# The sum S1 of two weight quadrants in a seven-product projection kernel: made on VectorE, or by an accumulating load

## The chip, the cores and the metric

The kernel runs on one core of a Trainium2 chip. The metric is device microseconds of one execution, the median of three runs.

## The reference, cut to what matters

One decoder layer: RMSNorm of `x`, one wide projection of it, four kinds of attention on parts of the projection, gates, four branch projections that are summed, an output projection and the residual. What matters for the change are the two large matrix products, with `w_in` (2048 x 20992) and with `w_out` (2048 x 2048):

```python
h = rms_norm(x, norm_g[l])
proj = jnp.einsum('bsd,de->bse', h, w_in[l])
(aq, ak, av, bq, bk, bv, cq, ck, cv, mq, za, zb, zc, zm, gates) = jnp.split(proj, split_at, axis=-1)
...
x = x + jnp.einsum('bsd,de->bse', merged, w_out[l])
```

## The kernel before

**Units.** Both products are done in units of 256 output columns, 82 for `w_in` and 8 for `w_out`; one call of `products` is one unit. A unit uses a scheme that needs seven block products instead of eight. Its weight is read as four quadrants of 128 x 1024 float32 (512 KB each): `a11`, `a21`, `a22`, `a12`. From these `wforms` makes the seven left operands: slot 1 is `a11`, slot 4 is S1 = `a21 + a22`, slot 5 is S1 minus `a11`, slot 6 is `a12` minus that, slot 0 is `a21 - a11`, slot 2 is `a12`, slot 3 is `a22`. S1 and its two successors are made in place in one buffer, so the operand for slot 4 has to be taken out before the one for slot 5 overwrites it, and so on.

**Split.** Each operand is split by `wsplit` into a rounded high part (ScalarE, line 135) and a low rest (VectorE, line 136). TensorE then does eight matmuls of the high part with 512 columns (line 612) and eight of the low part with 256 columns (line 615) for each slot. A slot of a unit is so 16 matmuls, a unit 112.

**Buffers.** The quadrants and S1 come from one pool of six buffers (`wraw`, `NW = 6`), five to a unit, handed out in turn. Each unit's S1 buffer is thus the one in which the unit before kept its `a12`, and it comes free when slot 2 of the unit before has been split. The split parts come from six buffers (`whl`, `NHL = 6`), so three splits may be ahead of TensorE.

**Queues.** The quadrants are loaded from SyncE's queue (line 579). GpSimd's queue carries the stores of results (`proj<-c` line 709, `gt<-c` and `sz<-c` line 720, `yz<-y` line 310, `out_dram<-c` line 801), some small loads, and short arithmetic of the attentions (`norms`, lines 247 to 251, and `rstd`, lines 148 and 149). VectorE also evacuates products (line 632), adds the parts of a result (line 651), scales gate columns (line 711) and adds the residual (line 800).

**Order.** The Tile framework's scheduler lays the instructions out engine by engine at build time, by priorities (`high_priority`) and its own timing model. At run time each engine goes through its list in order. Attention instructions stand among those of the units, so that TensorE has both.

Of the kernel before, what the change touches and what calls it, by code (L numbers as in the profile page):

```python
# [13 lines left out]
ALU = mybir.AluOpType  # L14
# [39 lines left out]
def trunk_kernel(ctx: ExitStack, tc: tile.TileContext, xT, xn, memT, memn, gains, wp, wmem,  # L54
                 wbA, wbB, wbC, wbM, wo, small_in, rows_in, tab, out):
    nc = tc.nc
    act, dve, pool, pe = nc.scalar, nc.vector, nc.gpsimd, nc.tensor
# [76 lines left out]
    def split(src, hi, lo):  # L134
        act.activation(hi, src, AF.Copy)  # L135
        dve.tensor_tensor(lo, src, hi.bitcast(F32), ALU.subtract)  # L136

    def wraw():
        return wst.tile([P, 1024], F32, name="wraw", bufs=NW)

    def wsplit(src):
        hi, lo = (wst.tile([P, 1024], F32R, name="whl", bufs=NHL) for _ in range(2))
        split(src, hi, lo)
        return hi, lo
# [429 lines left out]
    def wforms(src, early=False):  # L574

        with tc.high_priority(offset=AHEAD):
            a11, a21, a22, a12 = (wraw() for _ in range(4))
            for i, w in enumerate((a11, a21, a22, a12)):
                nc.sync.dma_start(w, src[:, i * 1024:(i + 1) * 1024])
            s1 = wraw()  # L580
            yield 1, wsplit(a11)
        with tc.high_priority(offset=AHEAD):
            dve.tensor_tensor(s1, a21, a22, ALU.add)  # L583
            dve.tensor_tensor(a21, a21, a11, ALU.subtract)  # L584
            yield 4, wsplit(s1)
        if early:
            with tc.high_priority(offset=AHEAD):
                yield 2, wsplit(a12)
        with tc.high_priority(offset=AHEAD):
            dve.tensor_tensor(s1, s1, a11, ALU.subtract)  # L590
            yield 5, wsplit(s1)
        with tc.high_priority(offset=AHEAD):
            dve.tensor_tensor(s1, a12, s1, ALU.subtract)  # L593
            yield 6, wsplit(s1)
        for slot_, w in ((0, a21), (2, a12), (3, a22)):
            if early and slot_ == 2:
                continue
            with tc.high_priority(offset=AHEAD):
                yield slot_, wsplit(w)

    def products(src, f, hq, last=None, phases=False, early=False):
# [7 lines left out]
        def mms(s, w, js, end):  # L609
# [4 lines left out]
            for j in js:  # L614
                pe.matmul(ps[:, 0:H], wl[:, j * P:(j + 1) * P], f[:, j, s, 0], start=False, stop=end and j == js[-1],  # L615
                          skip_group_check=s in (5, 6, 0, 3))

        ws = [v for v in wforms(src, early)]
        steps = [(v, range(8)) for v in ws]
        if early:  # L620
# [273 lines left out]
```

## Time and profile before

| what | value |
|---|---|
| median of 3 runs | 2290.77 us (2289.78 to 2290.8) |
| the profiled execution | 2289.92 us, its span 2288.1 us |
| granted TensorE clock, mean | 0.998 |
| TensorE busy | 2261.0 us, 99% |
| VectorE busy | 1870.5 us, 82% |
| ScalarE busy | 1273.8 us, 56% |
| GpSimd busy | 286.9 us, 13% |

The span is cut as follows: memory keys and the preparation of `x` up to about 61 us, the 82 units of `w_in` with the attentions among them up to about 1850 us, the branch projections, and the 8 units of `w_out` up to the end. In the profile an instruction is named by its line, engine, operation, the tile that it writes and those that it reads. "Idle before" is the time in which the engine had nothing to do just before the instruction, with what ended it.

### The profile page before, as it was taken

To read this page: it belongs to the slowest core of one execution; us is meant where nothing else is said; L and a number is where in the kernel's file an instruction comes from. 1 tells how busy PE (TensorE), PEld (TensorE's weight loads), DVE (VectorE), ACT (ScalarE), POOL (GpSimd) and SP (SyncE) were. 2 spreads that over 40 slices of the span, in tenths; PEclk is the share of its full clock that TensorE was granted. 3 is DMA by queue.
4 is the path that set the end of the run, shared out by engine and by line. 5 is a ranking of instruction groups with operands and counts; after the bars stand their busy time and mean duration, and the time that the engine had idled before them with its cause. 6 is when DMAs were issued, how large, how long until landed. Compare 5 with 4: busy or idle time off the path is not lost. (4 is left out here: it accounts for less than half of the span.)

```text
span 2288.1 us, 33763 instructions
## 1 busy us (share of the span) xinstructions
PE 2261.0 (99%) x12672; PEld 1951.3 (85%) x12672; DVE 1870.5 (82%) x2541; ACT 1273.8 (56%) x2253; POOL 286.9 (13%) x419
## 2 busy tenths in 40 slices
PE   9899999999999999999999999999999999999999
PEld 4788888888888888888888888888888888888888
DVE  5688899978887878888888888889888875578888
ACT  6646566675455456656666665656657542224444
POOL 2501011110011002111111201111021000010000
PEclk9999999999999999999999999999999999999999
DMA  8744444344443444444454434435344466485443
GB/s 302 231 139 139 138 151 158 125 143 133 139 129 118 131 165 135 157 130 152 141 158 135 153 125 157 137 128 159 111 157 137 144 214 215 157 278 176 138 164 113
DMA packets 114340, 355.43 MB, mean 155 GB/s; under 512 B 13744, under 2 KB 14256, under 8 KB 114176
## 3 DMA queue, kind: packets, MB, share of 16 engines
q1 hardware_dynamic: 95056, 287.89, 39.8%
q0 software_dynamic: 19120, 65.38, 7.7%
q8 instruction: 99, 1.62, 0.3%
q14 instruction: 65, 0.53, 0.1%
HBM read 294.47 MB, written 58.75 MB: 154 GB/s over the span
## 5 line engine op out<-in xcount | busy, mean ns | idle before, releaser
L612 PE MATMUL gbank<-f,whl 128*128 128x512 f32 x5040 | 1273.0, 396 | 15.5 <-ACT whl L135 10.6
L612 PEld LDWEIGHTS gbank<-f,whl 128*128 128x128 f32 x5040 | 913.7, 189 | 189.4 <-ACT whl L135 13.7
L135 ACT ACTIVATE whl<-wraw 128x1024 fp32r<-128x1024 f32 x678 | 706.2, 1057 | 497.0 <-PE gbank L612 159.6
L136 DVE TENSOR_TENSOR whl<-wraw,whl 128x1024 fp32r<-128x1024 f32 x678 | 821.2, 1220 | 167.0 <-ACT whl L135 161.4
L615 PEld LDWEIGHTS gbank<-f,whl 128*128 128x128 f32 x5040 | 677.3, 190 | 42.6 <-issue 1.0
L615 PE MATMUL gbank<-f,whl 128*128 128x256 f32 x5040 | 705.5, 284 | 0.0
L629 ACT ACTIVATE o<-gbank 128x512 f32<-128x512 f32 x270 | 159.8, 593 | 123.6 <-PE gbank L615 122.7
L632 DVE TENSOR_TENSOR o<-gbank,o 128x512 f32<-128x512 f32 x270 | 183.9, 686 | 27.0 <-PE gbank L615 19.9
L651 DVE TENSOR_TENSOR c<-o 128x512 f32<-128x512 f32 x179 | 132.5, 740 | 23.7 <-ACT o L634 23.4
L130 PE MATMUL gbank<-yz,whl 128*128 128x512 f32 x384 | 149.4, 389 | 0.0
L131 PE MATMUL gbank<-yz,whl 128*128 128x512 f32 x384 | 149.4, 389 | 0.0
L634 ACT ACTIVATE o<-gbank 128x512 f32<-128x512 f32 x89 | 52.8, 593 | 169.6 <-PE gbank L615 169.5
L132 PE MATMUL gbank<-yz,whl 128*128 128x512 f32 x384 | 147.0, 389 | 0.0
L583 DVE TENSOR_TENSOR wraw<-wraw 128x1024 f32<-128x1024 f32 x90 | 109.9, 1222 | 37.7 <-DMA wraw<-in_wp_dram 32.9
L593 DVE TENSOR_TENSOR wraw<-wraw 128x1024 f32<-128x1024 f32 x90 | 110.0, 1223 | 1.5
L590 DVE TENSOR_TENSOR wraw<-wraw 128x1024 f32<-128x1024 f32 x90 | 110.0, 1222 | 0.9
L584 DVE TENSOR_TENSOR wraw<-wraw 128x1024 f32<-128x1024 f32 x90 | 109.7, 1219 | 0.1
L131 PEld LDWEIGHTS gbank<-yz,whl 128*128 128x128 f32 x384 | 72.1, 188 | 15.1
L130 PEld LDWEIGHTS gbank<-yz,whl 128*128 128x128 f32 x384 | 72.1, 188 | 14.9
L132 PEld LDWEIGHTS gbank<-yz,whl 128*128 128x128 f32 x384 | 72.1, 188 | 14.8
L709 POOL DMA_DIRECT2D proj<-c x38 | 28.3, 746 | 442.8 <-DVE c L651 425.4
L720 POOL DMA_DIRECT2D gt<-c x32 | 24.5, 766 | 333.3 <-ACT c L718 282.9
(228 smaller groups left out, 1611.5 us busy)
## 6 DMA issues: line engine op xcount, KB each, us to landing
wraw<-in_wp_dram SPq DMA_DIRECT2D x328, 512.0 KB, 3.9
proj<-c POOLq DMA_DIRECT2D x38, 512.0 KB, 3.5
ld<-proj SPq DMA_DIRECT2D x76, 256.0 KB, 3.3
gt<-c POOLq DMA_DIRECT2D x32, 512.0 KB, 3.8
wraw<-in_wo_dram SPq DMA_DIRECT2D x32, 512.0 KB, 4.4
g<-gt SPq DMA_DIRECT2D x48, 256.0 KB, 4.0
wraw<-in_wmem_dram SPq DMA_DIRECT2D x16, 512.0 KB, 5.5
wraw<-in_wbB_dram SPq DMA_DIRECT2D x16, 512.0 KB, 4.2
```

The source lines that it names most:

```text
L130: pe.matmul(ps, ah, bh, start=first, stop=False)
L131: pe.matmul(ps, ah, bl, start=False, stop=False)
L132: pe.matmul(ps, al, bh, start=False, stop=last)
L135: act.activation(hi, src, AF.Copy)
L136: dve.tensor_tensor(lo, src, hi.bitcast(F32), ALU.subtract)
L590: dve.tensor_tensor(s1, s1, a11, ALU.subtract)
L593: dve.tensor_tensor(s1, a12, s1, ALU.subtract)
L612: pe.matmul(ps, wh[:, j * P:(j + 1) * P], f[:, j, s].rearrange("p a b -> p (a b)"), start=j == 0 and s in (1, 4, 2), stop=False, skip_grou ...
L615: pe.matmul(ps[:, 0:H], wl[:, j * P:(j + 1) * P], f[:, j, s, 0], start=False, stop=end and j == js[-1], skip_group_check=s in (5, 6, 0, 3))
L629: act.activation(q[{1: 0, 4: 3, 5: 1}[s]], ps, AF.Copy)
L632: dve.tensor_tensor(q[i], ps, q[i], ALU.add)
L651: dve.tensor_tensor(c, i0, i1, ALU.add)
```

## The change

S1 is no longer added up by VectorE from the two loaded quadrants. GpSimd loads `a21`'s columns a second time straight into the S1 buffer (the new line 581) and then `a22`'s columns a second time, with an accumulating load that adds them to what lies there (line 582). SyncE's four loads stay, since slots 0 and 3 need `a21` and `a22` by themselves. Later lines have numbers that are higher by one.

```diff
@@ -578,9 +578,10 @@
             for i, w in enumerate((a11, a21, a22, a12)):
                 nc.sync.dma_start(w, src[:, i * 1024:(i + 1) * 1024])
             s1 = wraw()
+            pool.dma_start(s1, src[:, 1024:2048])
+            pool.dma_start(s1, src[:, 2048:3072], accum_op=ALU.add)
             yield 1, wsplit(a11)
         with tc.high_priority(offset=AHEAD):
-            dve.tensor_tensor(s1, a21, a22, ALU.add)
             dve.tensor_tensor(a21, a21, a11, ALU.subtract)
             yield 4, wsplit(s1)
```

GpSimd's list before, in the columns of the A attention (`proj<-c` stores the result of a unit, the rows on `ssA` are the attention's arithmetic):

```order
L310 DMA yz<-y 128x512
L709 DMA proj<-c 128x2x512 x5
L247 TENSOR_TENSOR ssA<-ssA,r_101 128x8
L248 TENSOR_SCALAR ssA<-ssA 128x8
L250 TENSOR_TENSOR ssA<-ssA,hneg 128x8
L709 DMA proj<-c 128x2x512
L251 TENSOR_TENSOR ssA<-ssA,rA 128x8
```

The same engine and place in the changed kernel:

```order
L710 DMA proj<-c 128x2x512
L581 DMA wraw<-in_wp_dram 128x1024
L582 DMA wraw<-in_wp_dram 128x1024
L710 DMA proj<-c 128x2x512
L581 DMA wraw<-in_wp_dram 128x1024
L247 TENSOR_TENSOR ssA<-ssA,r_101 128x8
L248 TENSOR_SCALAR ssA<-ssA 128x8
L582 DMA wraw<-in_wp_dram 128x1024
L250 TENSOR_TENSOR ssA<-ssA,hneg 128x8
L251 TENSOR_TENSOR ssA<-ssA,rA 128x8
L710 DMA proj<-c 128x2x512
```

Between two stores there now stand the two loads of S1. Line 581 of a unit waits for VectorE's split of slot 2 of the unit before, line 582 for line 581's data. The store ahead of them is that of two units earlier, and in some units the attention's arithmetic stands between the two loads or behind them.

VectorE's list before, in the same columns, from line 590 of one unit to line 590 of the next:

```order
L590 TENSOR_TENSOR wraw<-wraw 128x1024
L651 TENSOR_TENSOR c<-o_5053 128x8x64
L136 TENSOR_TENSOR whl<-wraw,whl 128x1024
L593 TENSOR_TENSOR wraw<-wraw 128x1024
L136 TENSOR_TENSOR whl<-wraw,whl 128x1024 x3
L632 TENSOR_TENSOR o_5223<-gbank,o_5223 128x512
L136 TENSOR_TENSOR whl<-wraw,whl 128x1024
L583 TENSOR_TENSOR wraw<-wraw 128x1024
L632 TENSOR_TENSOR o_5223<-gbank,o_5223 128x512
L136 TENSOR_TENSOR whl<-wraw,whl 128x1024
L584 TENSOR_TENSOR wraw<-wraw 128x1024
L651 TENSOR_TENSOR c<-o_5222 128x8x64
```

The same stretch in the changed kernel, where line 591 was 590, 594 was 593, 585 was 584, 633 was 632 and 652 was 651:

```order
L591 TENSOR_TENSOR wraw<-wraw 128x1024
L652 TENSOR_TENSOR c<-o_5245 128x8x64
L136 TENSOR_TENSOR whl<-wraw,whl 128x1024
L594 TENSOR_TENSOR wraw<-wraw 128x1024
L585 TENSOR_TENSOR wraw<-wraw 128x1024
L136 TENSOR_TENSOR whl<-wraw,whl 128x1024 x3
L633 TENSOR_TENSOR o_5416<-gbank,o_5416 128x512
L136 TENSOR_TENSOR whl<-wraw,whl 128x1024 x2
L633 TENSOR_TENSOR o_5416<-gbank,o_5416 128x512
L633 TENSOR_TENSOR o_5415<-gbank,o_5415 128x512
L652 TENSOR_TENSOR c<-o_5416 128x2x256
L136 TENSOR_TENSOR whl<-wraw,whl 128x1024
```

The addition of line 583 is gone, and `a21 - a11` of the next unit (now line 585) has moved up behind line 594. The three rows of line 136 that follow it are slots 6, 0 and 2, the pair after them slot 3 and slot 1 of the next unit, and the last row slot 4 of the next unit.

## Rows read from the trace of the kernel before

**Rows 1.** The page: span, busy time and instructions of the engines.
```profile
span 2288.1 us, 33763 instructions
PE 2261.0 (99%) x12672; PEld 1951.3 (85%) x12672; DVE 1870.5 (82%) x2541; ACT 1273.8 (56%) x2253; POOL 286.9 (13%) x419
```
**Rows 2.** Waits of TensorE: who waited for whom, us in all, times, longest.
```profile
PE gbank L612 <- ACT whl L135: 10.6, 9, 2.9
PE gbank L612 <- ACT o L629: 4.6, 6, 2.1
```
**Rows 3.** Groups: line, engine, tiles, shapes, count; busy, mean ns; idle before.
```profile
L583 DVE TENSOR_TENSOR wraw<-wraw 128x1024 f32<-128x1024 f32 x90 | 109.9, 1222 | 37.7 <-DMA wraw<-in_wp_dram 32.9
...
L584 DVE TENSOR_TENSOR wraw<-wraw 128x1024 f32<-128x1024 f32 x90 | 109.7, 1219 | 0.1
```
**Rows 4.** Busy time in a stretch: TensorE's line 612 alone; all engines among w_out's units.
```profile
61.00:1845.00 1784.00, 1148.58 (x4537) 822.34 (x4538) 1.00 0.45 144
...
2156.00:2270.00 114.00, 114.00 (x655) 100.42 (x654) 100.78 (x101) 54.73 (x64) 4.68 (x7) 1.00 0.48 157
```
**Rows 5.** Timeline of ScalarE in w_out's units: start, us, operation, idle before it.
```profile
2208.14 1.06 ACT L135 ACTIVATE whl<-wraw 128x1024 fp32r<-128x1024 f32 x1 [1.31 <-DVE wraw L590]
...
2222.05 1.06 ACT L135 ACTIVATE whl<-wraw 128x1024 fp32r<-128x1024 f32 x1 [1.78 <-PE gbank L612]
```
**Rows 6.** Timeline of VectorE in w_out's units.
```profile
2206.82 1.22 DVE L590 TENSOR_TENSOR wraw<-wraw 128x1024 f32<-128x1024 f32 x1
2209.23 1.23 DVE L136 TENSOR_TENSOR whl<-wraw,whl 128x1024 fp32r<-128x1024 f32 x1 [1.19 <-ACT whl L135]
2210.49 1.23 DVE L593 TENSOR_TENSOR wraw<-wraw 128x1024 f32<-128x1024 f32 x1
...
2216.17 1.23 DVE L136 TENSOR_TENSOR whl<-wraw,whl 128x1024 fp32r<-128x1024 f32 x1 [0.33 <-ACT whl L135]
...
2220.05 1.22 DVE L583 TENSOR_TENSOR wraw<-wraw 128x1024 f32<-128x1024 f32 x1
...
2222.38 1.22 DVE L136 TENSOR_TENSOR whl<-wraw,whl 128x1024 fp32r<-128x1024 f32 x1
2223.51 1.22 DVE L584 TENSOR_TENSOR wraw<-wraw 128x1024 f32<-128x1024 f32 x1
```
**Rows 7.** DMA issues: queue, count, KB each, median us from issue to landing.
```profile
wraw<-in_wp_dram SPq DMA_DIRECT2D x328, 512.0 KB, 3.9
proj<-c POOLq DMA_DIRECT2D x38, 512.0 KB, 3.5
...
tabs<-in_tab_dram POOLq DMA_DIRECT2D x1, 512.0 KB, 8.2
```
**Rows 8.** DMA queues: packets, MB, share of 16 engines.
```profile
q1 hardware_dynamic: 95056, 287.89, 39.8%
```
**Rows 9.** Groups of the attentions and columns that stand among VectorE's splits; GpSimd's longest arithmetic.
```profile
L651 DVE TENSOR_TENSOR c<-o 128x512 f32<-128x512 f32 x179 | 132.5, 740 | 23.7 <-ACT o L634 23.4
...
L711 DVE TENSOR_TENSOR c<-c,Rb 128x1024 f32<-128x1024 f32 x44 | 53.8, 1222 | 0.7
...
L234 DVE CUSTOM_DVE_ANT_0 junk<-tk 128x128 f32<-128x128 f32 x88 | 25.3, 287 | 0.5
...
L250 POOL TENSOR_TENSOR ssA<-ssA,hneg 128x8 f32<-128x8 f32 x12 | 22.2, 1852 | 1.0
...
L264 DVE CUSTOM_DVE_ANT_1 E<-E,tabs 128x256 f32<-128x256 f32 x36 | 14.4, 420 | 0.2
```

## The prediction

> **What bounds the kernel now.** I read the page's first part, then TensorE's waits, then the busy time by stretches, then the timeline of a few units of `w_out`, where no attention stands between the matmuls. TensorE is busy 2261.0 of 2288.1 us [rows 1]. Its waits on the splits and on evacuations are 10.6 and 4.6 us in all [rows 2]: these 15.2 us are all that quicker splits could give back. Among the units of `w_out` TensorE works through the whole 114 us, 655 matmuls [rows 4], which is 655/112 = 5.85 units of **19.5 us**; no other engine can hold it up there. Among the units of `w_in` 4537 matmuls of line 612 in 1784 us [rows 4] are 4537/56 = 81.0 units of **22.0 us**, 2.5 us more than a bare unit, the attentions' matmuls. So TensorE's work is the limit, and VectorE's is under it. What counts is how near another loop of waits comes to 19.5 or 22.0 us.
>
> **What is removed.** 90 additions of line 583 at 1222 ns, 109.9 us of VectorE [rows 3]. VectorE is busy 100.78 of 114 us where TensorE never waits [rows 4], so this work lies beside TensorE's, and taking it away gives at most the 15.2 us of [rows 2]. The waits for the quadrants that line 583 now bears (37.7 us idle before it [rows 3]) go over to line 585, which is the first to need `a21`.
>
> **What is added, on the engine that issues.** Two GpSimd issues per unit, 180 in all. GpSimd is busy 13% [rows 1], so the issues themselves are hidden. But GpSimd goes in order. Line 582 waits for line 581's data, and behind it are queued the store of the last unit's result (not urgent: its buffer is written again only after slot 0 of the next unit, five of seven slots on) and, in some units, the attention's arithmetic, for which ScalarE and then TensorE wait. More 512 KB transfers are 94.4 MB (180 x 0.524) beside 287.89 MB that take 39.8% of the DMA engines' time on SyncE's queue [rows 8]: about 13 points more at the same price, some 20 if each accumulated byte is paid twice. Bandwidth is not the limit.
>
> **What is added, on the way to S1.** Before, S1 exists 1.22 us after both quadrants lie there. An example: VectorE ends slot 2's split at 2217.40 (2216.17 + 1.23) and S1 is ready at 2221.27 (2220.05 + 1.22) [rows 6]; ScalarE's split of slot 4 follows at 2222.05 and it did not wait for S1 but for TensorE, 1.78 us [rows 5]. Now line 581 can't begin before slot 2's split has freed the buffer, so the two transfers come one after the other in that very gap. With X for the plain load and Y for the accumulating one, the split of slot 4 comes X + Y after the split of slot 2, plus handoffs.
>
> This closes a **loop** that doesn't pass through TensorE. From S1's landing: split of slot 4, S1 minus `a11`, split of slot 5, `a12` minus that, and then, by VectorE's list, `a21 - a11` of the next unit and the low parts of slots 6, 0 and 2; then line 581 of the next unit, line 582, and S1 lands again. Its steps, from starts in the timeline: ScalarE's high part to VectorE's low part 1.09 (2208.14 to 2209.23); low part to the next subtraction in the same buffer 1.26 (2209.23 to 2210.49); subtraction to the next high part 1.32 (2206.82 to 2208.14) [rows 5, 6]; VectorE instructions in a row 1.13 (2222.38 to 2223.51) [rows 6]. The sum is 1.09 + 1.26 + 1.32 + 1.09 + 1.26 + 4 x 1.13 + 1.23 = **11.8 us**. Three handoffs (slot 2 to line 581, to line 582, to ScalarE) at 0.10 each, which is what lies between line 590's end at 2208.04 and ScalarE's start at 2208.14 [rows 5, 6], make 12.1. The adding up of a result (line 651, 740 ns [rows 9]) fits in the 1.19 us in which VectorE waits for slot 5's high part [rows 6].
>
> **X and Y.** X is nearest to SyncE's load of the same quadrant, median 3.9 us; GpSimd's own 512 KB stores take 3.5 [rows 7]. I take 3.9. For Y the trace has no accumulating load. Its lower bound is a 512 KB store, 3.5; nothing excludes that price, but an add in flight has no reason to be quicker than a plain transfer. Its upper bound is the slowest 512 KB load from GpSimd, 8.2, at the start among much other traffic [rows 7]. In between: the destination has to be read too. By [rows 8] 16 engines at 39.8% of 2288.1 us moved 287.89 MB, 19.8 GB/s each, so 512 KB on 16 engines is 1.66 us of pure transfer; a second reading of that size gives 3.9 + 1.7 = 5.6, which I take, since it is the plain row plus the one thing that is known to be added. X + Y = 9.5, and the loop is 12.1 + 9.5 = **21.6 us**, against 19.5 in a bare unit. It would be hidden only for X + Y up to 7.4.
>
> The trace's own price for such a load is 3.9 us [rows 7]. The Trainium skill, DMA: Bandwidth & Descriptors, section Anatomy of one DMA, fits GpSimd's transfers as 2.0 us plus bytes over 436 GB/s, an estimate of 3.2 us for 512 KB, which this trace's loads exceed. The Trainium skill, Collectives: The Full Stack, section on the bandwidth ceiling, says that a reducing transfer is slower because it reads two sources and not because of the addition; with the fit that would be an estimate of 4.4 us for Y, 7.6 for both and a loop of 19.7, at the edge of being hidden, and this is the third rival's case.
>
> **The sum.** I counted by VectorE's list what else stands in each unit between slot 4's and slot 2's low parts. In 30 of the first 81 units it is 1.8 us or less: a bare unit. There the loop is 21.6 against 19.5: 30 x 2.1 = 63 us. In 51 units gate scaling (1222 ns) and the attentions' steps (287, 420 ns and the like [rows 9]) add 4.3 us on average, of which 1.3 fits in the gap: a loop of 24.6. These units took (81.0 x 22.0 - 30 x 19.5)/51 = 23.5 us before, so 1.1 more on average; since both lengths vary by 2 us and more from unit to unit and a unit takes the longer, I add 0.6, which is my choice: 51 x 1.7 = 87. In `w_out` the residual (line 800) lies in the loop and adds about 0.6: 22.2 against 19.5, 7 x 2.7 = 19. Together 169 us on the profiled execution's 2289.92 (its span and 1.8 us around it), which is 0.85 under the median of 2290.77. **Forecast 2460 us**, 7.4% slower.
>
> **Rivals.**
> (1) *The accumulating load is dear*: Y = 8.2. Then the loop is 24.2 in bare units, 27.2 with attentions, 24.8 in `w_out`: 30 x 4.7 + 51 x 3.7 + 7 x 5.3 = 367, **2658 us**. For it: read, modify and write of 512 KB on the same 16 engines as SyncE's four loads. Against: the 8.2 is one row from the kernel's crowded start.
> (2) *It costs what a plain load costs*, Y = 3.9: loops of 19.9, 22.9 and 20.5. Bare units 30 x 0.4, `w_out` 7 x 1.0, attentions 51 x 0.4 for the uneven ones: 39 us, **2330 us**. What then shows more is GpSimd's order: I count 14 units in which the attention's arithmetic is caught between lines 581 and 582 or just behind; each may wait 3.9 us, at most 55 us if TensorE has nothing else in its list. By either the time is 2330 to 2345.
> (3) *Other side: the loop is hidden.* If X + Y is 7.4 or less (both at the 3.5 of GpSimd's stores give 7.0 and a loop of 19.1), no unit gets longer and the 110 us off VectorE shorten the waits of TensorE on splits and evacuations, 15.2 us at most: **2276 us**. It decides by X + Y alone. Half of it, or an X + Y just at the edge, is no change.
> (4) *The change doesn't do what it says*: VectorE might still wait for both quadrants at the same point, since line 585 needs `a21`. It waits for one quadrant, which is loaded as before; S1 no longer depends on it. I give it nothing of its own.
>
> **How the numbers follow.** Forecast, Y between about 4.5 and 7: 0.50. Rival 1: 0.20. Rival 2: 0.16. Rival 3: 0.14, of which 0.06 no change and 0.08 faster. Slower by over 0.2% is 0.50 + 0.20 + 0.16 = 0.86; 0.2%, some 5 us, is about what a measurement of this kernel can tell from no change. The range leaves out the gain of rival 3 and the end of rival 1: 2290 to 2640; the forecast's own range, Y from 4.5 to 7 at 88 units x 1 us for each us, is 2360 to 2580.
>
> **What would show it.** Right: ScalarE's split of slot 4 (line 135) waits for a DMA into `wraw` in most units; TensorE's waits on line 135 grow from 10.6 to over 100 us; the distance from VectorE's split of slot 2 to line 135 on S1 is X + Y + 0.3; landing of line 582 is over 4.5 us. VectorE's busy time falls by 110 us and TensorE's share falls to some 92%. Wrong: if both landings add up to under 7.4 us, or if line 581 goes out well before slot 2's split ends. If bare units are as long as before and those with attentions are not, it was GpSimd's order.

## The result, and the profile after

The changed kernel takes **2750.97 us** (median; 2741.71 to 2767.41) where the kernel before takes 2290.78 (2289.78 to 2295.73): a ratio of **1.2014, 95% interval 1.199 to 1.2038**, 460 us slower. The forecast was 2460 us with a range up to 2640. Its direction and its mechanism hold, its size does not. The profiled execution has a span of 2746.1 us.

The page's first part, in the columns of [rows 1]:

```profile
span 2746.1 us, 34151 instructions
PE 2407.3 (88%) x12672; PEld 2032.6 (74%) x12672; DVE 1784.2 (65%) x2451; ACT 1265.7 (46%) x2253; POOL 398.3 (15%) x599
```

VectorE has lost 86 us of busy time, as wanted (added up one by one its instructions fall by 110 us, but they overlap a little where they stand in a row), and nothing is gained by it: TensorE now stands idle for 338.8 us (2746.1 - 2407.3) where it was 27.1. Whom it waits for stands in its waits (who waited for whom, us in all, times, longest), the answer to [rows 2], and below it who ScalarE and GpSimd wait for:

```profile
PE gbank L613 <- ACT whl L135: 280.2, 155, 12.4
...
ACT whl L135 <- DMA wraw<-in_wp_dram: 512.2, 80, 11.2
...
POOL wraw L581 <- DVE whl L136: 474.0, 66, 66.1
POOL wraw L582 <- DMA wraw<-in_wp_dram: 334.0, 73, 8.0
```

Read upward, these four lines are the loop. Line 582 waits for line 581's data; ScalarE's high part waits for the data of both in 80 of the 82 units of `w_in`; TensorE waits for ScalarE, 280.2 us where it was 10.6; and line 581 waits for VectorE's split of slot 2 of the unit before.

One unit without attention, on GpSimd and on ScalarE (start, us, engine, line, operation, idle time before it and what ended it):

```profile
626.67 0.56 POOL L581 DMA_DIRECT2D wraw<-in_wp_dram  x1 [7.23 <-DVE whl L136]
631.81 0.88 POOL L582 DMA_DIRECT2D wraw<-in_wp_dram  x1 [4.58 <-DMA wraw<-in_wp_dram]
642.52 0.75 POOL L710 DMA_DIRECT2D proj<-c  x1 [9.84 <-DVE c L652]
650.43 0.56 POOL L581 DMA_DIRECT2D wraw<-in_wp_dram  x1 [7.16 <-DVE whl L136]
...
637.53 1.06 ACT L135 ACTIVATE whl<-wraw 128x1024 fp32r<-128x1024 f32 x1 [9.04 <-DMA wraw<-in_wp_dram]
```

The three pieces of the loop can be read off the starts: x, line 581 to line 582, 631.81 - 626.67 = 5.14 us; y, line 582 to the split of slot 4, 637.53 - 631.81 = 5.72; z, that split to the next unit's line 581, 650.43 - 637.53 = 12.90. Together 23.76 us, where the forecast had 21.6 for such a unit and TensorE's matmuls need 19.5 [rows 4].

VectorE in the same unit, from the low part of slot 4 on:

```profile
638.62 1.22 DVE L136 TENSOR_TENSOR whl<-wraw,whl 128x1024 fp32r<-128x1024 f32 x1 [5.80 <-ACT whl L135]
639.88 1.23 DVE L591 TENSOR_TENSOR wraw<-wraw 128x1024 f32<-128x1024 f32 x1
641.02 1.10 DVE L652 TENSOR_TENSOR c<-o 128x512 f32<-128x512 f32 x1
642.28 1.22 DVE L136 TENSOR_TENSOR whl<-wraw,whl 128x1024 fp32r<-128x1024 f32 x1 [0.17 <-ACT whl L135]
643.54 1.22 DVE L594 TENSOR_TENSOR wraw<-wraw 128x1024 f32<-128x1024 f32 x1
644.79 1.23 DVE L585 TENSOR_TENSOR wraw<-wraw 128x1024 f32<-128x1024 f32 x1
645.93 1.22 DVE L136 TENSOR_TENSOR whl<-wraw,whl 128x1024 fp32r<-128x1024 f32 x1
647.66 2.36 DVE L136 TENSOR_TENSOR whl<-wraw,whl 128x1024 fp32r<-128x1024 f32 x2 [0.51 <-ACT whl L135]
```

The last row holds the low parts of slots 0 and 2. It ends at 650.02, and line 581 follows at 650.43: GpSimd takes 0.41 us after VectorE's end, where the forecast had taken 0.10 for such a handoff.

The landings of the two loads (us from issue to landing, minimum, median, maximum), line 581 first, then line 582, then SyncE's quadrant loads of line 579:

```profile
L581 POOL DMA_DIRECT2D wraw<-in_wp_dram x82: 533/564/625, 58.8 to 2240.8; - x82
DMA to landing us min/median/max: 3.8/5.0/8.4
...
L582 POOL DMA_DIRECT2D wraw<-in_wp_dram x82: 867/892/950, 67.7 to 2245.9; - x82
DMA to landing us min/median/max: 5.1/5.5/10.1
...
L579 SPq DMA_DIRECT2D wraw<-in_wp_dram x328: 327/328/1050, 46.3 to 2239.3; - x164
DMA to landing us min/median/max: 3.4/4.2/7.7
```

The first row also gives the length of a unit: line 581 is issued 82 times from 58.8 to 2240.8 us, so 81 units of (2240.8 - 58.8)/81 = **26.94 us** on average, where it was 22.0. That is 4.94 x 81 = 400 us. In `w_out` four issues of line 581 stand 25.4 us apart where it was 19.5, 7 x 5.9 = 41 us. These 441 us are nearly all of the 458 by which the span has grown.

### The profile page after: what moved, and what is told of

Same layout as the page of the kernel before. It is cut to its first block, busy times and chain, and to the rows that moved or that the text cites. A ratio compares the mean times of both kernels' runs of the same rounds, so it can differ in the third digit from the quotient of the medians.

```text
span 2746.1 us, 34151 instructions
## 1 busy us (share of the span) xinstructions
PE 2407.3 (88%) x12672; PEld 2032.6 (74%) x12672; DVE 1784.2 (65%) x2451; ACT 1265.7 (46%) x2253; POOL 398.3 (15%) x599
## 5 line engine op out<-in xcount | busy, mean ns | idle before, releaser
L613 PE MATMUL gbank<-f,whl 128*128 128x512 f32 x5040 | 1365.6, 417 | 304.3 <-ACT whl L135 280.2
L613 PEld LDWEIGHTS gbank<-f,whl 128*128 128x128 f32 x5040 | 962.5, 199 | 531.4 <-ACT whl L135 317.1
L135 ACT ACTIVATE whl<-wraw 128x1024 fp32r<-128x1024 f32 x678 | 704.4, 1057 | 1097.6 <-DMA wraw<-in_wp_dram 512.2
L616 PEld LDWEIGHTS gbank<-f,whl 128*128 128x128 f32 x5040 | 693.8, 195 | 50.8 <-DVE whl L136 5.9
L616 PE MATMUL gbank<-f,whl 128*128 128x256 f32 x5040 | 714.6, 287 | 1.9 <-DVE whl L136 1.8
L630 ACT ACTIVATE o<-gbank 128x512 f32<-128x512 f32 x270 | 158.2, 589 | 118.5 <-PE gbank L616 118.0
L585 DVE TENSOR_TENSOR wraw<-wraw 128x1024 f32<-128x1024 f32 x90 | 110.2, 1224 | 36.7 <-DMA wraw<-in_wp_dram 27.8
L582 POOL DMA_DIRECT2D wraw<-in_wp_dram x82 | 73.6, 897 | 361.2 <-DMA wraw<-in_wp_dram 334.0
L581 POOL DMA_DIRECT2D wraw<-in_wp_dram x82 | 46.8, 571 | 485.4 <-DVE whl L136 330.0
L591 DVE TENSOR_TENSOR wraw<-wraw 128x1024 f32<-128x1024 f32 x90 | 110.0, 1222 | 1.9
L594 DVE TENSOR_TENSOR wraw<-wraw 128x1024 f32<-128x1024 f32 x90 | 109.8, 1220 | 1.1
```

What stands on the lines that cost most here:

```text
L613: pe.matmul(ps, wh[:, j * P:(j + 1) * P], f[:, j, s].rearrange("p a b -> p (a b)"), start=j == 0 and s in (1, 4, 2), stop=False, skip_grou ...
L630: act.activation(q[{1: 0, 4: 3, 5: 1}[s]], ps, AF.Copy)
```

## The experiments

Three explanations were set against each other: the **loop** through S1's buffer, as forecast; the **queue or traffic**, that is GpSimd's order and the 94 MB more; and a **dear accumulating load**. Diffs are against the changed kernel unless another is named. The length of a unit is worked out as above, from the first and last issue of S1's first load. Where no interval is given there is one time, and the changed kernel's own four times lie up to 26 us apart; the kernel before ran between 2285 and 2297 us beside all of them.

**S1 in buffers of its own.** The six raw buffers are divided: one or two for S1, the rest for the quadrants. The other weights, which used the same pool, take turns in both; these lines are left out of the diff.

```diff
+    def s1raw():
+        return wst.tile([P, 1024], F32, name="s1raw", bufs=1)   # second run: 2
-        return wst.tile([P, 1024], F32, name="wraw", bufs=NW)
+        return wst.tile([P, 1024], F32, name="wraw", bufs=NW - 1)   # NW - 2
-            s1 = wraw()
+            s1 = s1raw()
```

> S1 gets one buffer of its own and the quadrants the other five, so line 581 (here 590) waits for the split of slot 6 of its own last S1 instead of slot 2 of the unit before: two VectorE splits earlier, about 2.3 us. Loop theory (the two transfers stand in series in a loop that is longer than TensorE's work): each of 89 units gets about 2.3 us shorter, bare units of 24 us go to 21.5 to 22, total about 2540 us (2500 to 2580). Queue and traffic theory (GpSimd's order, or the added bytes, are what costs): the same issues and bytes, so about 2750 us.

> S1 gets two buffers and the quadrants four, six in all as before. Line 581 (here 590) then waits for an S1 of two units earlier, so both transfers have a whole unit of time. Loop theory: the loop is gone, TensorE bounds again, 2275 to 2320 us, and the granted clock is back at 0.99 to 1.00. Queue and traffic theory: the same 180 issues and 94 MB from GpSimd, still slower than 2600 us.

With two buffers 2343.8 us, ratio 1.0229 (1.0212 to 1.0246), 24 us over the range expected by the loop and far from the queue's: 407 of the 460 us are gone with the same loads, bytes and queues. With one buffer 2644.1 us, units of 25.75 us: more than expected by the loop, less than by the queue. The reason came out of the next four runs.

**Moving S1 in the ring.** The tiles take buffers in the order in which the code first writes them, and the buffer that came free first is taken first. For each unit five come free in turn: by slot 3's split (of the unit before the last), then in the unit before by S1 minus `a11`, by slot 6's split, slot 0's and slot 2's. With the change S1 is written fifth and gets the last of these; the quadrants get the other four. Where S1's loads stand among the quadrant loads therefore decides which release S1 waits for, and the traces of all five orders show these releases. (The section on the kernel before has the buffers go round in the tiles' own order; the traces show that they go by which came free first.)

```diff
+            s1 = wraw()
             a11, a21, a22, a12 = (wraw() for _ in range(4))
             for i, w in enumerate((a11, a21, a22, a12)):
+                if i == 0:                        # 0, 1, 2 or 3
+                    pool.dma_start(s1, src[:, 1024:2048])
+                    pool.dma_start(s1, src[:, 2048:3072], accum_op=ALU.add)
                 nc.sync.dma_start(w, src[:, i * 1024:(i + 1) * 1024])
-            s1 = wraw()
-            pool.dma_start(s1, src[:, 1024:2048])
-            pool.dma_start(s1, src[:, 2048:3072], accum_op=ALU.add)
```

> The six raw weight buffers are handed out in the order in which their first writes stand in the code. Here the two loads of S1 stand ahead of the four quadrant loads instead of behind them: S1 then takes the buffer that the third quadrant (a22) of the unit before the last one left, instead of that of the previous unit's second-last split. Loads, bytes, queues and arithmetic are those of the change. If the loop through the buffer is the loss, it is gone with a whole unit of slack: 2276 to 2345 us, TensorE's wait for the weight split under 20 us. If the loss is the queue, the traffic or the accumulating load itself: 2650 us or more.

> The same with the two loads of S1 behind the first quadrant's load: S1 takes the first quadrant's (a11) buffer of the previous unit, which is free once the subtraction ahead of slot 5's split has read it. Loop: three steps of about 1.2 us shorter than with the change, so about 3.6 us less per unit over 81 units, 2330 to 2480 us, 2460 taken. Queue or traffic: 2700 to 2770 us.

> The same with the two loads of S1 behind the second quadrant's load: S1 takes its own buffer of the previous unit, free after slot 6's split. Loop: two steps of about 1.2 us shorter, about 2.4 us less per unit over 81 units, so about 2555 us (2500 to 2610). Queue or traffic: 2700 to 2770 us.

> The same with the two loads of S1 behind the third quadrant's load: S1 takes the second quadrant's (a21) buffer of the previous unit, free after slot 0's split. Loop: one step of about 1.2 us shorter, about 1.2 us less per unit over 81 units, so about 2650 us (2610 to 2700). Queue or traffic: 2700 to 2770 us.

| S1's loads wait for | us | unit, us | expected by the loop |
|---|---|---|---|
| slot 2's split, unit before (the change) | 2751.0 | 26.94 | |
| slot 0's split | 2757.8 | 27.11 | 2650 |
| slot 6's split | 2638.8 | 25.80 | 2555 |
| the subtraction ahead of slot 5's split | 2416.3 | 23.27 | 2460 |
| slot 3's split, a unit earlier | 2309.5 | 22.13 | 2276 to 2345 |

The last has a ratio of 1.0086 (1.0068 to 1.0104), and its page reads almost like that of before:

```profile
span 2305.9 us, 34093 instructions
PE 2262.2 (98%) x12672; PEld 1950.6 (85%) x12672; DVE 1774.3 (77%) x2451; ACT 1271.6 (55%) x2253; POOL 413.7 (18%) x599
...
PE gbank L614 <- ACT whl L135: 4.3, 6, 1.9
```

So **the 460 us hang on the place in the ring**: same instructions, same 180 loads, same accumulation, 2751 or 2309. Queue, traffic and accumulation as such cost 19 us where the loop has slack. One thing moves along: the scheduler lays VectorE's list anew, and in the last two rows of the table the next unit's `a21 - a11` stands behind slot 0's split or later in nearly all units, where in the first three it stands just ahead of or behind line 594, among the loop's steps. This is one step of 1.2 us a unit. With S1 a unit earlier ScalarE's splits wait for a load in 2 units of `w_in`, 4.5 us in all, where it was 80 units and 512.2 us, so there it is the slack that opens the loop and not the order.

The steps in between are not the even ones of the loop theory: the first brings nothing, and its time lies in the range that the queue was given, the second 119 us, the third 222. The landings say why for the first two. Line 582 where S1 waits for slot 6's split, then with S1's single buffer of its own, which is the same release:

```profile
L582 POOL DMA_DIRECT2D wraw<-in_wp_dram x82: 863/899/961, 55.7 to 2145.8; - x82
DMA to landing us min/median/max: 5.4/8.0/11.0
...
DMA to landing us min/median/max: 5.2/8.1/11.6
```

And lines 581 and 582 in one unit of `w_out` where S1 waits for slot 0's split:

```profile
2612.07 0.56 POOL L581 DMA_DIRECT2D wraw<-in_wo_dram  x1 [7.07 <-DVE whl L136]
2619.66 0.87 POOL L582 DMA_DIRECT2D wraw<-in_wo_dram  x1 [7.04 <-DMA wraw<-in_wo_dram]
```

Here x, from line 581 to line 582, is 7.59 us instead of 5.14. SyncE's quadrant loads are released by the other four of the five releases. Issued one step earlier, S1's loads run beside more of them (on average x is 6.47 instead of 5.84, y, from line 582 to the split of slot 4, 6.48 instead of 5.89, which eats the 1.04 us won in z, 14.18 instead of 15.22); issued two steps earlier, it is the accumulating load above all that does, with 8.0 us instead of 5.5: counted from issues and landings, 2.8 quadrant loads are under way at some time during it on average, where with the change it is 0.9. This is also why the single buffer of its own, 2644 us, came out with the run at 2639: it is the same wait and the same collision.

The third step is another thing: where S1 waits for the subtraction, the split of slot 4 waits for S1's load in only 2 of the units of `w_in`. What comes late there is a quadrant, `a21`, whose load now goes out one release later, at slot 6's split, and whose subtraction stands in VectorE's way (27.8 us of this wait with the change):

```profile
DVE wraw L586 <- DMA wraw<-in_wp_dram: 225.7, 74, 6.2
```

The 2416 us are therefore no longer S1's loop, and that they lie near the 2460 expected by it is luck.

**The parts of the two loads.** Only the second quadrant loaded by GpSimd, the third added by VectorE; then the second load without its addition, which leaves the sum out (S1 is `a22` alone).

```diff
-            pool.dma_start(s1, src[:, 2048:3072], accum_op=ALU.add)
+            dve.tensor_tensor(s1, s1, a22, ALU.add)      # ahead of line 585
```
```diff
-            pool.dma_start(s1, src[:, 2048:3072], accum_op=ALU.add)
+            pool.dma_start(s1, src[:, 2048:3072])
```

> GpSimd loads only a21 into S1's buffer; VectorE adds a22 there. Buffers as in the changed kernel. One transfer of about 5 us less in the loop, one addition of 1.2 us more: loop theory says 4.4 us less per unit, bare units at 19.5 to 20, total 2310 to 2380 us. If the wait for the freed buffer alone were the cost, and not the length of what follows it, most of the 460 us would stay: over 2600 us.

> The second load of S1 is plain instead of accumulating; the addition is left out, S1 is a22 alone. All waits and buffers stay. Loop theory with the landings seen in the changed kernel (5.0 us plain, 5.5 us accumulating): about 0.5 us less per unit, 2690 to 2740 us. If the accumulation in flight were what is dear (two readings on the same engines, slowing SyncE's loads too), the time falls by 150 us or more, under 2600 us.

With one load 2391.2 us, 11 over the range expected: the second load carries 360 of the 460 us. With a plain second load 2620.6 us; it lands in 3.9 us (median), the accumulating one in 5.5, and the unit is 25.51 us:

```profile
DMA to landing us min/median/max: 3.7/3.9/10.8
```

The accumulation therefore costs 26.94 - 25.51 = 1.43 us a unit, and with 1.6 for each of the 7 units of `w_out`, the difference of the landings, 1.43 x 81 + 7 x 1.6 = 127 of the 130 us measured. Both expectations of this run miss. The loop's range of 2690 to 2740 took the plain second load at the 5.0 us of the first; with 3.9 the loop gives what was measured, and the prediction's own difference of the two prices, 1.7 us, was about right. The dear load in its strict form is not borne out: SyncE's loads land no sooner without the accumulation (median 4.4 us, with it 4.3). But 130 of the 460 us are the accumulation's, through the loop.

**The first load on the other queue.**

```diff
-            pool.dma_start(s1, src[:, 1024:2048])
+            nc.sync.dma_start(s1, src[:, 1024:2048])
```

> The change with the first load of S1 issued by SyncE instead of GpSimd; the accumulating one stays. With the change the first load takes 5.84 us from its issue to the next on average over the 81 units, where SyncE's loads of the kernel before landed in 3.9. If GpSimd's queue makes it slow, it lands in about 4 here and the unit is 1 to 1.9 us shorter: 2600 to 2670 us. If it is slow because the quadrant loads are under way at the same time, SyncE has nothing over GpSimd: 2700 to 2790 us, and the loads of SyncE show a landing above 4.3.

2762.6 us, no gain. The load lands no sooner when SyncE issues it:

```profile
L581 SPq DMA_DIRECT2D wraw<-in_wp_dram x82: 327/328/532, 59.9 to 2252.5; - x82
DMA to landing us min/median/max: 3.5/5.2/8.3
```

So it is not GpSimd's queue that makes it 5.0 instead of the 3.9 of [rows 7]. What is left is when it is issued: from either queue 2.7 quadrant loads are under way during it on average.

**One step of the loop longer.** An operation of 1.2 us that leaves the tile as it is, once with the change, once with S1 a unit earlier in the ring.

```diff
             dve.tensor_tensor(s1, a12, s1, ALU.subtract)
+            dve.tensor_tensor(s1, s1, s1, ALU.max)
             yield 6, wsplit(s1)
```

> The change with one more DVE operation (the larger of S1's tile and itself, which leaves it as it is, 1.1 to 1.2 us) between the subtraction and the split of slot 6, a step of the loop. If every microsecond in a step comes back once per unit: 1.13 us by 81 and 7 units, about 99 us, so 2850 us (2830 to 2865). If DVE's idle time takes it up, because the loop is closed by the loads or by TensorE: 2750 to 2780 us.

> The same operation where S1's loads stand ahead of the quadrants' (2309.5 us without it). The loop has a whole unit of slack there and DVE is busy 77% of the span: 2305 to 2335 us. If the operation costs its time whatever the loop does: about 2400 us.

Both miss: 2936.1 us (185 more, twice the forecast) and 2363.6 (54 more). VectorE in the first of them, to be laid beside the unit above:

```profile
663.43 1.22 DVE L594 TENSOR_TENSOR wraw<-wraw 128x1024 f32<-128x1024 f32 x1
664.59 1.22 DVE L585 TENSOR_TENSOR wraw<-wraw 128x1024 f32<-128x1024 f32 x1
665.73 1.22 DVE L595 TENSOR_TENSOR wraw<-wraw 128x1024 f32<-128x1024 f32 x1
668.07 1.23 DVE L136 TENSOR_TENSOR whl<-wraw,whl 128x1024 fp32r<-128x1024 f32 x1 [1.12 <-ACT whl L135]
```

Line 595 is the new operation. It starts 2.30 us after line 594, not 1.15: VectorE's list has the next unit's `a21 - a11` (line 585) in between. With the change alone that subtraction stands at the same place but costs nothing, because it runs (644.79) while ScalarE makes slot 6's high part. With the new operation ScalarE must wait for both. z becomes 17.60 us on average, 2.38 more, which is the 2.30; x is 0.5 shorter and y 0.2 longer, and the unit is 29.13, 2.19 more, or 178 of the 185 us over 81 units. So what comes into the chain does come back in every unit, and here what had been covered came in with it. In the second run 0.6 us a unit is paid even with a unit of slack. TensorE waits 33.3 us for line 135 there instead of 4.3; that slot 6's split comes later after slot 5's, a distance that no buffer hides, would account for it, but this is argued and not measured.

**What is left with S1 a unit earlier.** S1 added by VectorE in the first four units; then the first load on SyncE's queue; and, as a control for the two buffers of its own, the kernel before with four and two. The diff is of the first, against the run with S1 a unit earlier (`unit = [0]` stands further up and is left out).

```diff
+            unit[0] += 1
+            dma = unit[0] > 4
-                if i == 0:
+                if dma and i == 0:
+            if not dma:
+                dve.tensor_tensor(s1, a21, a22, ALU.add)
```

> S1's loads ahead of the quadrants' as in the run with a whole unit of slack (2309.5 us), but in the first four units S1 is made by DVE as in the kernel before. In that run TensorE lost 11 us more than before within the first 300 us, where the DMA share is highest. If that is the startup traffic, this gives 2294 to 2302 us; if the rest is spread over all units by the traffic, 2303 to 2312 us. A gain over the kernel before (under 2286) would need TensorE's 27 us of idle time in the whole span to shrink.

> S1's loads ahead of the quadrants' and the first of them issued by SyncE, in all units. With a whole unit of slack nothing waits for S1, so SyncE's queue decides: the plain load stands ahead of the next unit's a11 there and waits for a buffer that is free early. 2295 to 2320 us by the loop theory; over 2400 if SyncE's queue gets held up.

> The kernel before (S1 added on DVE, no extra load) with the buffers split into four for the quadrants and two for S1, as in the second run. If that run's remaining 52 us are the split's, this gives 2320 to 2345 us; if they are the extra loads' traffic, 2289 to 2300 us.

The first gives 2298.3 us, ratio 1.0035 (1.0021 to 1.0048): the first four units, at the crowded start, account for 11 of the 19 us, as expected. The second gives 2325.6, 6 us over its range; what these 6 us are was not found, and one time can't tell them from chance. The control gives 2359.1, over its range of 2320 to 2345: dividing the buffers costs the kernel before 68 us by itself. That is more than the 53 us left over with two buffers of its own, so the loads need not be called on for these; since the control is 15 us slower than the run with the loads, the two costs don't simply add, and how the 53 divide is not shown. None of the versions is faster than the kernel before. TensorE has 27 us of idle time there to win, and the best variant does not get below it (it has 40).

## Why the prediction was right and wrong

**Right: bound, chain and order of things.** ScalarE's split of slot 4 waits for a DMA in 80 units, TensorE's waits on line 135 went from 10.6 to 280.2 us, the landing of line 582 is over 4.5 us (5.5), and line 581 goes out when slot 2's split ends. The steps named in the forecast are the steps in the trace, and the runs that open the loop (2309 and 2344) show that they carry the time. Rival 3 (X + Y of 7.4 or less) and rival 2 (a plain load's price) did not come about; rival 1's time of 2658 was passed without its cause, since Y is not 8.2. TensorE's share was to be some 92% and is 88%.

**Wrong: the sizes of X and of the loop's other steps.** X was put at 3.9 us and the steps at 14.0 a unit; they measured 5.84 and 15.22. The averages over the units of `w_in`, made from the issues of lines 581 and 582 and the starts of ScalarE's split as in the unit above (y and z over the 79 units in which that split waits for the data):

| piece | forecast, us | measured, us | x 81 |
|---|---|---|---|
| x, plain load | 3.9 | 5.84 | +157 |
| y, accumulating load | 5.6 | 5.89 | +24 |
| z, the steps | 12.1, and 3.0 in 51 units: 14.0 | 15.22 | +100 |
| unit | 23.5 | 26.94 | +280 |

The forecast's three handoffs of 0.10 stand in its z, though two of them belong to x and y.

With `w_out` (25.4 instead of 22.2, 7 x 3.2 = 22) that is 302 us. The forecast's own sum for `w_in`, 63 + 87 = 150, was 29 above 81 x (23.5 - 22.0), because units are uneven and take the longer of loop and matmuls; and 17 of the 458 us lie outside the units counted here. 302 - 29 + 17 = 290, of the 291 by which it fell short.

The largest is **X**. The forecast took the median of SyncE's loads in the kernel before [rows 7]. These start 4.9, 7.7, 7.3 and 1.5 us after one another (medians), with 0.8 others of their kind under way on average; the fourth, close behind the third, took 4.9 us already there. Line 581 is issued in the very stretch in which the previous unit's splits give SyncE its buffers, with 2.7 quadrant loads under way during it. The range covered it only through Y; for X the text has a single value, and that was the mistake: the row was for loads of the same size, but of another moment. The medians differ by 1.1 us (5.0 against 3.9), and slow landings bring the average to 5.3. The rest of x is a second handoff on GpSimd: line 582 starts 0.40 us after the landing in the median, 0.53 on average, where the forecast had 0.10. GpSimd's other work, rival 2's fear, holds line 582 back by 2 us or more in the first two units and in one later one.

**Y** was well sized: 1.6 us over the plain second load (5.5 against 3.9), where the forecast had set a second reading at 1.66. No run takes the reading apart from the adding, so the reason given fits and is not shown. It also holds for a load with little beside it, as here; two steps earlier in the ring the same load took 8.0. The Trainium skill, Collectives: The Full Stack, section on the bandwidth ceiling, puts the price of a reducing transfer, there a step of a ReduceScatter, on its second read and not on the addition; the size of the difference, 1.6 us, agrees with it. The Trainium skill's fit in DMA: Bandwidth & Descriptors, section Anatomy of one DMA, by which Y was estimated at 4.4 us, is 1.1 too low here.

In **z** the forecast counted VectorE's extra instructions by its list and missed the rest. In the unit without attention z is 12.90 instead of 12.1 (11.9 without the two handoffs): 0.31 is GpSimd's handoff, and 0.60 comes in between the low parts of slots 6 and 0, which start 1.73 us apart (645.93 and 647.66) and not 1.13, since ScalarE's high part comes later. In units with attention ScalarE's work stands in the loop as well. One of them, z 16.23 us, on VectorE and ScalarE:

```profile
1822.46 1.23 DVE L591 TENSOR_TENSOR wraw<-wraw 128x1024 f32<-128x1024 f32 x1
1823.60 0.68 DVE L239 TENSOR_TENSOR tk<-tk,ssC 128x512 f32<-128x512 f32 x1
1824.20 0.68 DVE L652 TENSOR_TENSOR c<-o 128x512 f32<-128x512 f32 x1
1824.92 1.23 DVE L712 TENSOR_TENSOR c<-c,Rb 128x1024 f32<-128x1024 f32 x1
1826.06 1.22 DVE L136 TENSOR_TENSOR whl<-wraw,whl 128x1024 fp32r<-128x1024 f32 x1
...
1831.07 1.05 ACT L135 ACTIVATE whl<-wraw 128x1024 fp32r<-128x1024 f32 x1
1832.02 1.13 ACT L258 ACTIVATE V<-abank,R 128x128 f32<-128x128 f32 x4
1833.02 0.65 ACT L263 ACTIVATE E<-abank,ssC 128x128 f32<-128x128 f32 x2
1833.51 1.10 ACT L135 ACTIVATE whl<-wraw 128x1024 fp32r<-128x1024 f32 x1
```

VectorE takes 3.60 us from line 591 to the next low part (2.40 in the unit above), and ScalarE puts 1.4 us of attention (1833.51 less the end at 1832.12) between the splits of slots 0 and 2. The forecast counted the first kind and not the second.

What stays open is the make-up of the 100 us in z. It holds everything from ScalarE's split to the next load, waits for TensorE's products and buffers among it, and no run separated ScalarE's share, VectorE's and these. The plain second load and the longer step show only that what is added to x + y + z comes back one for one.

## What to carry to other kernels

Before a load takes an operation's place, ask which release its buffer waits for and draw the loop from that release back to itself: a load that is free with a unit of slack costs its full latency in every unit when its buffer comes free only just ahead of its use, and here the place of one tile in the ring decided between 0.9% and 20%. Price such a load by what else is released at that moment, not by the median of loads issued ahead, and then count everything that stands in the in-order queues between the steps, on every engine of the loop. When a step gets longer, look for what had been covered beside it.

## What the hardware showed

TensorE ran slower after its waits. TensorE in the unit above, then four stretches of two units, ahead of and behind the split of slot 4 (start and end, length, busy us with count, granted clock as a share of 2.4 GHz, DMA share, GB/s):

```profile
633.74 2.00 PE L613 MATMUL gbank<-f,whl 128*128 128x512 f32 x8
635.58 1.11 PE L616 MATMUL gbank<-f,whl 128*128 128x256 f32 x8
638.64 2.93 PE L613 MATMUL gbank<-f,whl 128*128 128x512 f32 x8 [1.94 <-ACT whl L135]
641.36 1.88 PE L616 MATMUL gbank<-f,whl 128*128 128x256 f32 x8
...
626.70:637.50 10.80, 9.99 (x60) 1.00 0.70 190
637.50:650.40 12.90, 11.76 (x55) 0.87 0.37 128
650.40:661.90 11.50, 9.73 (x58) 1.00 0.66 177
661.90:674.80 12.90, 11.82 (x56) 0.87 0.38 129
```

After an idle time of 1.94 us eight matmuls take 2.93 us instead of 2.00 and the next eight 1.88 instead of 1.11, and the granted clock of that stretch is 0.87, so part of it at the lower of its two levels, 1.2 GHz. TensorE's busy time is 146 us longer in all (2407.3 against 2261.0). It is first of all a consequence: with S1 a unit earlier in the ring TensorE is busy 2262.2 us. A little of it reaches the loop. In this unit the evacuation ahead of ScalarE's split of slot 0 waits 0.22 us for TensorE:

```profile
646.09 0.60 ACT L630 ACTIVATE o<-gbank 128x512 f32<-128x512 f32 x1 [0.22 <-PE gbank L616]
```

How much of the 460 us comes back this way in all units was not measured.

An accumulating load also occupies GpSimd longer when it is issued, 0.89 us against 0.53 for the plain one at the same place. And loads that are under way together slow each other: line 582 lands in 5.5 us with 0.9 quadrant loads beside it and in 8.0 with 2.8, and SyncE's quadrant loads land in 5.1 us with S1 a unit earlier in the ring, 3.9 in the kernel before, with the DMA engines not full on average (the two queues' shares are 38.6% and 26.2%).
